# Attention: a tile's transposed probabilities gathered in SBUF, its products with V in one run beside the modulation's

## The chip, the cores and the metric

The kernel runs on one core of one Trainium2 chip. The metric is the device time of one execution in microseconds. The core has a matrix engine (TensorE, PE in the profile; PEld is its loading of the stationary operand), a vector engine (VectorE, DVE), a scalar engine (ScalarE, ACT), GpSimd (POOL) and SyncE (SP), which here issues DMAs. Matrix products land in PSUM, which has eight banks of 128 x 512 fp32; from there VectorE and ScalarE copy results to SBUF.

## The reference, cut to what matters

The program is one step of a diffusion transformer with two layers, on 128 context tokens and 1024 latent tokens. The part that the change touches is the attention of a layer and, beside it, the modulation, a product of the two conditioning vectors with a wide matrix.

```python
def block_attention(q, k, v):              # 8 heads, q and k 96 wide, v 64 wide
    def one_block(qi):                     # 128 queries at a time
        s = jnp.einsum('bqhd,bkhd->bhqk', qi, k).astype(F32) * scale
        p = jax.nn.softmax(s, axis=-1).astype(v.dtype)
        return jnp.einsum('bhqk,bkhd->bqhd', p, v)
...
def layer(x, cond, lp, rope=None, ctx=None):
    mod = (jax.nn.silu(cond) @ lp['w_ada'] + lp['b_ada'])[:, None, :]
    sh1, sc1, g1, sh2, sc2, g2 = jnp.split(mod, N_MOD, axis=-1)
    h = rmsnorm(x, lp['g_mix']) * (1 + sc1) + sh1
    comb = h @ lp['w_in']
    attn, ckv, kr = mla_mixer(comb[..., :MLA_IN], lp, rope, None if ctx is None else ctx[:2])
    ...
    mixed = jnp.concatenate([attn, ssm, conv], axis=-1)
    x = x + g1 * (mixed @ lp['w_out'])
```

Context queries see the 128 context keys alone; latent queries see 128 cached and 1024 latent keys. The scan (`ssm`) and a long convolution over 31 tokens (`conv`) are the other two mixers of the layer.

## The kernel before

The kernel holds the 1152 tokens in three chunks of 384, features on the partitions. A layer runs its input projections and the scan, then the attention, the output projection and the feed-forward part. Accurate products are made of three matmuls in a reduced fp32 format (`mm3`, lines 103 to 105: high by high, high by low, low by high); the products with V, the modulation's and the transposes are plain fp32.

The attention runs over four pairs of heads (`i`) and, in each, nine tiles of 128 queries (`t`). Tile 0 holds the context queries and has one block of 128 keys; the other eight, called full here, have three blocks of 384 keys (nine times 128). For each of the two heads of a pair (`j`), `scores` makes the blocks of scores in banks of the tag "A" (five), takes their maximum on VectorE (line 806), joins the maxima (808) and scales them (809), and writes the exponentials with their sums to `P` on ScalarE (811). `attend`, run for a tile while the next one's scores are made, takes the keys two times 128 at a time: it transposes the four blocks of P on TensorE (832) to a bank "T" (two), copies them to `pt` on ScalarE or VectorE (837 and 839), and multiplies them with V into the only bank "V" (843), both heads side by side on 64 columns each. At its end a product with ones (854) spreads the reciprocal sums, and VectorE scales the result into `mo` (857), which goes to DRAM.

Spread over the tiles of layer 0 are the steps of the modulation (`adas`, line 166): a load of 512 KB of w_ada on SP's queue into a ring `ws` of three buffers, two steps ahead of its use, and eight products of 32 columns (186), whose results are added up in `ms` on VectorE. They show in the trace as 16 passes, as each plain fp32 product takes two; a product with V does too. The taps of the long convolution (`conv_taps`) run on GpSimd through both attentions, and `conv_norm` (line 875; its first matmuls are on line 881) reads their result from tile 25 on. `prep_k`, `prep_v`, `prep_r` and `prep_q` make a pair's keys, values and queries from the latents.

The calls stand in the loops in one order, but the framework schedules: each engine's queue is filled from what is ready by the framework's own estimate of time, the work that is earlier in the text first. On the chip every queue then runs strictly in that order. So a step of the modulation, for example, is cut in two where an older product becomes ready.

Of the kernel before, what the change touches and what calls it, by code (L numbers as in the profile page):

```python
# [8 lines left out]
F32 = mybir.dt.float32  # L9
# [8 lines left out]
KD = 8  # L18
# [35 lines left out]
def build(tc, nc, ap, dbg=None):  # L54
# [109 lines left out]
    KO = (0, 4, 1, 5, 2, 6, 3, 7)  # L164

    def adas(rounds, stage=None, ahead=2):
        """128 columns of each of a round's four quarters at a time; loads run ahead of the products"""
        stage = stage or wp
        steps = [(l, r, q, k) for l, r in rounds for q in range(4) for k in range(0, KD, 2)]
        loads = []  # L170
        m = None
        for n in range(len(steps) + ahead):
            if n < len(steps):
                l, r, q, k = steps[n]
                loads.append(stage.tile([128, 1024], F32, tag="ws", name="ws", bufs=ahead + 1))
                Q.dma_start(loads[-1], ap["w_ada"][l, r, q, k // 2])
            if n >= ahead:
                l, r, q, k = steps[n - ahead]
                st = loads.pop(0)
                if k == 0:  # L180
                    m = sm.tile([128, 128], F32, tag="ms", name="ms", bufs=2)
                b = bank("A")
                for kk in range(2):
                    for j in range(4):
                        o = 512 * kk + 128 * j
                        PE.matmul(b[32 * j:32 * j + 32, :128], cond[:, k + kk, :], st[:, o:o + 128],
                                  start=kk == 0, stop=kk == 1)
                if k:
                    add_to(V, m, b[:, :128], m)
                else:  # L190
                    copy(m, b[:, :128])
                if k == KD - 2:
                    ada_end(l, r, q, m)
            yield
# [25 lines left out]
    def norm_r(x, p, sqs=None):  # L220
        """1 / rms of the chunk's tokens on every partition; sqs: room for all squares, summed on TensorE"""
# [72 lines left out]
    first = adas([(0, 0)], sp, 6)  # L294
# [15 lines left out]
    for l in range(L):  # L310
# [6 lines left out]
        def h_terms(c, w):  # L317
            """stationary weights [k, cols], moving h chunk"""
# [4 lines left out]
        # ================= in projection: x, B, C of the scan =================  # L323
# [17 lines left out]
        for c in range(NC3):  # L341
# [34 lines left out]
        # lowest: what the attention's first tiles can take over soonest  # L376
# [6 lines left out]
        # ================= state-space scan =================  # L383
        # dt = softplus(.), log1p(e) = 2 atanh(e / (2 + e))
# [89 lines left out]
        def ssd_out():  # L474
# [12 lines left out]
            for c in range(9):  # L487
                o = xcol(c)
                # dt of the pairs of tokens in each direction's range
# [13 lines left out]
                # a direction's exponents are 0 outside of its range  # L503
# [10 lines left out]
                if c == 8:  # L514
                    # the long convolution's products would hold up the scan on this engine
# [39 lines left out]
        # ================= in projection: conv module =================  # L555
# [28 lines left out]
        def latent(c):  # L584
            """chunk c's query latent (high and low part, halves), key latent (high and low part), rotary key"""
# [35 lines left out]
        def token_tail(c, tns, ss):  # L621
            # rotary key part
# [57 lines left out]
        def latents():  # L680
            # cached keys
# [27 lines left out]
        def prep_v(r, cs=range(NC3)):  # L709
# [3 lines left out]
            for c in cs:  # L713
                ck = lat[c][1]
                for t in range(KC[c][0] // 128, KC[c][1] // 128):
                    b0 = bank("A")
                    o = 128 * t - KC[c][0]
                    mm3(b0[:, :256], [(ck[:, 0, o:o + 128], ck[:, 1, o:o + 128],
                                       w[0][:, 512 + 256 * r:768 + 256 * r], w[1][:, 512 + 256 * r:768 + 256 * r])])
                    copy(vt[r][:, t], b0[:, :256])  # L720

        def prep_k(i, cs=range(NC3)):
            w = lat["w"][0]
            for c in cs:
                a, b = KC[c]
                b0 = bank("A")
# [15 lines left out]
        # ================= attention =================  # L742
        qr = {}

        def prep_r(r, cs=range(NC3)):
            if r not in qr:
                qr[r] = at.tile([128, T], F32, tag="qr", name="qr", bufs=1)
            for c in cs:
                tb = [at.tile([128, CH], F32, tag="tb", name="tb", bufs=4) for _ in range(2)]
                for n in range(2):  # L750
                    Q.dma_start(tb[n], ap["rf"][:, c, n])
                    b0 = bank("A")
                    o = 512 * n + 128 * r
                    mm3(b0[:, :CH], [(wr[0][:, o + 256 * k:o + 256 * k + 128], wr[1][:, o + 256 * k:o + 256 * k + 128],
                                      lat[c][0][:, 0, k], lat[c][0][:, 1, k]) for k in range(2)])
                    V.tensor_mul(tb[n], tb[n], b0[:, :CH])
                add_to(V, qr[r][:, CH * c:CH * c + CH], tb[0], tb[1])
# [4 lines left out]
        prep_r(0, (0, 1))  # L762
        prep_k(0, (2,))
        prep_v(0, (2,))
        prep_r(0, (2,))
# [19 lines left out]
        class Tile_:  # L785
            """one tile of queries of a pair of heads"""

            def __init__(self, i, t, q, mo):
                self.i, self.t, self.q, self.mo = i, t, q, mo
                self.sl = small(8, "sl", 3)  # L790
                self.prs = []

            def scores(self, j):
                """exp of a head's scores, less their maximum, and the sums"""
                t, q, sl = self.t, self.q[j], self.sl
                o = 128 * (t % 3)
                blocks = [(0, 128)] if t == 0 else [(128 + CH * b, CH) for b in range(3)]
                n = len(blocks)
# [3 lines left out]
                for b, (k0, w) in enumerate(blocks):  # L802
# [4 lines left out]
                if n > 1:  # L807
                    V.reduce_max(mx[:, 3:4], mx[:, 0:3], axis=AX.X)
                V.tensor_scalar_mul(mx[:, 3:4], mx[:, 3:4] if n > 1 else mx[:, 0:1], -SCALE)  # L809
                for b, (k0, w) in enumerate(blocks):  # L810
                    S.activation(pr[:, CH * b:CH * b + w], bs[b][:, :w], AF.Exp, bias=mx[:, 3:4], scale=SCALE,  # L811
# [369 lines left out]
```

## Time and profile before

| what | us |
|---|---|
| median of 3 runs | 3323.62 |
| lowest and highest of them | 3323.19, 3326.77 |
| span of the profiled execution | 3325.1 |
| of it: layer 0's attention, first score to the output projection (346.9 to 763) | 416.1 |
| of it: layer 1's attention (2005 to 2360) | 355.0 |

The span of the profiled execution, from its first to its last instruction, lies within the three runs and 1.5 us above their median. In the rows further down, a row of the timeline gives the start of an instruction, or of a merged run of equal ones (x8 is eight), and the modelled time up to the end of the last. Matmuls overlap in the array, so their durations exceed the distance between their starts; what one costs is the distance from its start to the start of the next.

### The profile page before, as it was taken

The numbers are of one execution on the slowest core, as the hardware profiler recorded it, in microseconds if no ns is written. First come the engines' busy times: TensorE is split into PE (matmuls) and PEld (weight loads), VectorE is DVE, ScalarE is ACT, GpSimd is POOL, SyncE is SP. The second block draws the span as 40 slices with busy tenths as digits, with TensorE's granted clock in tenths as the row PEclk, the third lists the DMA queues.
The fourth block names the chain that finished last, engine by engine and source line by source line (L and its number), as shares of the span: only waits on it lengthen the run. The fifth ranks groups of instructions, "written<-read, shape, count | busy, mean of one in ns | idle before, by whom it ended". The sixth has DMA issues, their size and how long they took to land. (4 is left out here: it accounts for less than half of the span.)

```text
span 3325.1 us, 50558 instructions
## 1 busy us (share of the span) xinstructions
PE 3123.8 (94%) x20610; PEld 2900.9 (87%) x20610; DVE 1856.9 (56%) x3811; ACT 1081.1 (33%) x2461; POOL 1183.7 (36%) x699
## 2 busy tenths in 40 slices
PE   6995799999999999999999957999999999999998
PEld 5974667779999999999999746777899999999997
DVE  6779876663733333333386798777463333333335
ACT  4433455563411111111143334667431111111113
POOL 2457994012412112111233579672232212112112
PEclk7997899999999999999999978999999999999998
DMA  6100333334111111111121010000311111111111
GB/s 233 54 24 31 115 113 122 125 132 146 29 48 45 45 39 45 45 39 39 51 100 54 24 49 18 11 17 30 137 39 39 45 45 45 45 39 45 45 32 58
DMA packets 67000, 202.36 MB, mean 61 GB/s; under 512 B 7888, under 2 KB 25424, under 8 KB 65232
## 3 DMA queue, kind: packets, MB, share of 16 engines
q1 hardware_dynamic: 63456, 194.02, 17.5%
q10 hardware_dynamic: 3312, 5.11, 0.4%
q8 instruction: 162, 2.65, 0.3%
q14 instruction: 70, 0.57, 0.1%
HBM read 177.44 MB, written 21.66 MB: 60 GB/s over the span
## 5 line engine op out<-in xcount | busy, mean ns | idle before, releaser
L81 POOL TENSOR_TENSOR wl<-ws,wh 128x1024 fp32r<-128x1024 f32 x164 | 399.1, 2440 | 1581.0 <-ACT wh L84 1508.5
L103 PE MATMUL psA<-hh,wh 128*128 128x384 f32 x2496 | 836.6, 337 | 4.4 <-ACT hh L270 2.7
L104 PE MATMUL psA<-hl,wh 128*128 128x384 f32 x2496 | 837.5, 336 | 0.4 <-DVE hl L271 0.4
L105 PE MATMUL psA<-hh,wl 128*128 128x384 f32 x2496 | 837.5, 336 | 0.0
L103 PEld LDWEIGHTS psA<-hh,wh 128*128 128x128 f32 x2496 | 471.4, 189 | 8.5 <-ACT hh L270 3.9
L104 PEld LDWEIGHTS psA<-hl,wh 128*128 128x128 f32 x2496 | 471.6, 189 | 2.2 <-DVE hl L271 1.1
L105 PEld LDWEIGHTS psA<-hh,wl 128*128 128x128 f32 x2496 | 471.3, 189 | 0.3
L998 DVE TENSOR_TENSOR fs<-fs,psA 128x384 f32<-128x384 f32 x132 | 72.9, 554 | 666.5 <-PE psA L105 657.6
L78 POOL TENSOR_TENSOR acc<-ct,acc 128x1167 f32<-128x1167 f32 x120 | 326.5, 2720 | 9.8
L84 ACT ACTIVATE wh<-ws 128x1024 fp32r<-128x1024 f32 (+1 forms) x178 | 184.5, 1049 | 414.7 <-PE psA L104 197.4
L997 ACT ACTIVATE fs<-psA 128x384 f32<-128x384 f32 x132 | 63.8, 485 | 655.6 <-PE psA L105 655.6
L1051 DVE SCALAR_TENSOR_TENSOR x<-psT,mod,x 128x384 f32<-128x384 f32 (+1 forms) x320 | 157.7, 513 | 198.6 <-PE psT L105 198.6
L811 ACT ACTIVATE P<-psA,mx 128x384 f32<-128x384 f32 (+1 forms) x400 | 224.1, 571 | 132.8 <-DVE mx L809 87.8
L806 DVE TENSOR_REDUCE mx<-psA 128x1 f32<-128x384 f32 (+1 forms) x400 | 209.0, 540 | 78.2 <-PE psA L105 75.7
L1051 DVE SCALAR_TENSOR_TENSOR x<-psA,mod,x 128x384 f32<-128x384 f32 (+2 forms) x384 | 186.8, 513 | 53.4 <-PE psA L105 46.9
L1001 DVE TENSOR_TENSOR fl<-fs,fh 128x384 fp32r<-128x384 f32 x132 | 167.5, 1270 | 65.7 <-ACT fh L84 65.7
L843 PE MATMUL psV<-pt,vv 128*64 128x128 f32 x2336 | 191.5, 285 | 5.4 <-DVE pt L837 2.8
L832 PE MATMUL psT<-cst,P 128*128 128x128 f32 x1168 | 193.9, 287 | 2.4 <-DVE mod L203 1.0
L104 PE MATMUL psA<-fl,wh 128*128 128x384 f32 x576 | 193.2, 335 | 0.0
L105 PE MATMUL psA<-fh,wl 128*128 128x384 f32 x576 | 193.0, 335 | 0.0
L103 PE MATMUL psA<-fh,wh 128*128 128x384 f32 x576 | 189.9, 337 | 2.7 <-DVE fs L998 2.7
L103 PE MATMUL psA<-K,q 128*128 128x384 f32 (+1 forms) x400 | 160.6, 402 | 28.2 <-ACT P L811 21.5
(267 smaller groups left out, 6020.1 us busy)
## 6 DMA issues: line engine op xcount, KB each, us to landing
ws<-w_ada SPq DMA_DIRECT2D x96, 512.0 KB, 3.4
ws<-w_gate SPq DMA_DIRECT2D x44, 512.0 KB, 3.6
ws<-w_up SPq DMA_DIRECT2D x44, 512.0 KB, 3.5
ws<-w_down SPq DMA_DIRECT2D x44, 512.0 KB, 3.5
x<-xT SPq DMA_DIRECT2D x6, 1536.0 KB, 7.8
ws<-w_fm SPq DMA_DIRECT2D x16, 512.0 KB, 3.4
ws<-w_out SPq DMA_DIRECT2D x16, 512.0 KB, 3.6
mf<-mixed SPq DMA_DIRECT2D x18, 384.0 KB, 5.7
```

The lines of the kernel that those rows point to most:

```text
L78: eng.tensor_tensor(out, a, b, ALU.add)
L81: eng.tensor_tensor(out, x, hi.bitcast(F32), ALU.subtract)
L84: S.activation(out, x, AF.Copy)
L103: PE.matmul(out, sh, mh, start=i == 0, stop=False)
L104: PE.matmul(out, sh, ml, start=False, stop=False)
L105: PE.matmul(out, sl, mh, start=False, stop=i == n - 1)
L806: V.reduce_max(mx[:, b:b + 1], b0[:, :w], axis=AX.X)
L811: S.activation(pr[:, CH * b:CH * b + w], bs[b][:, :w], AF.Exp, bias=mx[:, 3:4], scale=SCALE, accum_out=sl[:, 3 * j + b:3 * j + b + 1])
L832: PE.transpose(tb[:, 256 * u + 128 * j:256 * u + 128 * j + 128], prs[j][:, 128 * (a + u):128 * (a + u) + 128], ident)
L843: PE.matmul(ob[64 * j:64 * j + 64, :128], vv[:, kt, 64 * h:64 * h + 64], pt[:, 256 * u + 128 * j:256 * u + 128 * j + 128], start=kt == kts ...
L1001: V.tensor_sub(fl[:, sl], sg, fh[:, sl].bitcast(F32))
L1051: V.scalar_tensor_tensor(X[c][:, m, a:b], b0[:, a:b], modT[l][:, 40 + m, s:s + 1], X[c][:, m, a:b], ALU.mult, ALU.add)
```

## The change

`attend` is parted. `turn` makes the 18 transposes of a full tile in five groups and keeps them all in one buffer `pt` (128 x 2 x 1152); its groups are placed behind the second and third score block of each head of the next tile, and what is left of it behind that tile's scores. Then `attend` makes the tile's 36 passes with V and the sums' product, which now writes columns 256 to 383 of the same bank "V". `P` has three buffers for four, `pt` one for three smaller ones.

`adas` takes two loads and 16 products a step in the attention (40 steps for 80), issues the next loads behind the products, and is called behind `attend`: twice at every third tile, once at the others. `prep_q` for a pair's first chunk comes at the last tile of the pair before, `prep_r(1)` in three parts in pair 1, `prep_v` copies two tiles from one bank. Comments are dropped. Cut to its core:

```diff
-    def adas(rounds, stage=None, ahead=2):
+    def adas(rounds, stage=None, ahead=1, per=2):
+        steps = [(l, r, q, k) for l, r in rounds for q in range(4) for k in range(0, KD, 2 * per)]
...
+        def load(l, r, q, k):
+            bufs = 3 if stage is None else ahead + 1
+            sts = [(stage or wp).tile([128, 1024], F32, tag="ws", name="ws", bufs=bufs) for _ in range(per)]
+            for i, st in enumerate(sts):
+                Q.dma_start(st, ap["w_ada"][l, r, q, k // 2 + i])
+            loads.append(sts)
...
+            for kk in range(2 * per):
+                for j in range(4):
+                    o = 512 * (kk % 2) + 128 * j
+                    PE.matmul(b[32 * j:32 * j + 32, :128], cond[:, k + kk, :], sts[kk // 2][:, o:o + 128],
+                              start=kk == 0, stop=kk == 2 * per - 1)
...
+            if stage is None and n + ahead < len(steps):
+                load(*steps[n + ahead])
...
-    first = adas([(0, 0)], sp, 6)
+    first = adas([(0, 0)], sp, 6, 1)
...
-                pr = at.tile([128, T], F32, tag="P", name="P", bufs=4)
+                pr = at.tile([128, T], F32, tag="P", name="P", bufs=3)
...
+            def turn(self):
+                self.pt = at.tile([128, 2, T], F32, tag="pt", name="pt", bufs=1)
+                todo = [(j, u) for u in range(len(self.kts)) for j in range(2)]
+                pt = self.pt.rearrange("p j (u q) -> p u j q", q=128)
+                for a in range(0, len(todo), 4):
+                    part = todo[a:a + 4]
+                    tb = bank("T")
+                    for n, (j, u) in enumerate(part):
+                        PE.transpose(tb[:, 128 * n:128 * n + 128], self.pr[j][:, 128 * u:128 * u + 128], ident)
...
+                    if a % 8:
+                        V.tensor_copy(o, src)
+                    else:
+                        copy(o, src)
+                    yield
             def attend(self):
...
+                for u, kt in enumerate(self.kts):
+                    for j in range(2):
+                        h = 2 * (i % 2) + j
+                        PE.matmul(ob[64 * j:64 * j + 64, :128], vv[:, kt, 64 * h:64 * h + 64],
+                                  self.pt[:, j, 128 * u:128 * u + 128], start=u == 0, stop=u == n - 1)
...
                 for j in range(2):
-                    PE.matmul(rb[64 * j:64 * j + 64, :128], ones[:, 0:64], dl[:, j], start=True, stop=True)
+                    PE.matmul(ob[64 * j:64 * j + 64, 256:384], ones[:, 0:64], self.dl[:, j], start=True, stop=True)
...
                     cur = Tile_(i, t, qs[i, c], mo)
-                    cur.scores(0)
...
-                    next(ag, None)
-                    next(prev, None)
-                    cur.scores(1)
-                    next(ag, None)
-                    drain(prev)
-                    prev = cur.attend()
+                    for j in range(2):
+                        for b, _ in enumerate(cur.scores(j)):
+                            if b:
+                                next(turn, None)
+                    drain(turn)
+                    if prev:
+                        prev.attend()
+                    for _ in range(2 if t % 3 == 0 else 1):
+                        next(ag, None)
+                    prev, turn = cur, cur.turn()
                     if t == 3 * c and c + 1 < NC3:
                         qs[i, c + 1] = prep_q(i, c + 1)
-                    if t % 2:
-                        next(ag, None)
+                    if i == 1 and t >= 5 and t < 8:
+                        prep_r(1, t - 5)
+                    if t == 8 and i + 1 < NPAIR:
+                        qs[i + 1, 0] = prep_q(i + 1, 0)
```

## Rows read from the trace of the kernel before

**Rows 1.** The page's part 1: busy time, share of the span and instructions.

```profile
PE 3123.8 (94%) x20610; PEld 2900.9 (87%) x20610; DVE 1856.9 (56%) x3811; ACT 1081.1 (33%) x2461; POOL 1183.7 (36%) x699
```

**Rows 2.** Busy time by stretch: stretch, length, engines' busy us, granted clock, DMA.

```profile
346.90:763.00 416.10, 391.75 (x3995) 299.68 (x3995) 296.33 (x763) 228.55 (x652) 195.17 (x97) 0.98 0.37 127
...
2005.00:2360.00 355.00, 325.95 (x2695) 265.65 (x2695) 269.90 (x671) 224.81 (x632) 199.65 (x98) 0.98 0.08 28
```

**Rows 3.** TensorE's timeline, layer 1: start us, modelled us, instruction, count.

```profile
2253.64 1.09 PE L843 MATMUL psV<-pt,vv 128*64 128x128 f32 x16
2254.67 0.66 PE L832 MATMUL psT<-cst,P 128*128 128x128 f32 x4
2255.26 0.66 PE L843 MATMUL psV<-pt,vv 128*64 128x128 f32 x8
2255.84 0.44 PE L832 MATMUL psT<-cst,P 128*128 128x128 f32 x2
...
2256.30 0.33 PE L104 MATMUL psA<-K,q 128*128 128x384 f32 x1
2256.47 0.33 PE L105 MATMUL psA<-K,q 128*128 128x384 f32 x1
...
2257.51 0.34 PE L105 MATMUL psA<-K,q 128*128 128x384 f32 x1
2257.77 0.66 PE L843 MATMUL psV<-pt,vv 128*64 128x128 f32 x8
2258.26 0.39 PE L854 MATMUL psT<-dl,ones 128*64 128x128 f32 x4
...
2258.80 1.09 PE L832 MATMUL psT<-cst,P 128*128 128x128 f32 x8
2259.65 0.42 PE L103 MATMUL psA<-K,q 128*128 128x384 f32 x1
...
2260.62 0.34 PE L105 MATMUL psA<-K,q 128*128 128x384 f32 x1
2260.80 0.60 PE L832 MATMUL psT<-cst,P 128*128 128x128 f32 x4
2261.15 0.48 PE L103 MATMUL psA<-lat,wh 128*128 128x512 f32 x1
```

**Rows 4.** The same view, layer 0, where modulation stands beside V.

```profile
678.60 0.66 PE L843 MATMUL psV<-pt,vv 128*64 128x128 f32 x8
679.19 0.64 PE L186 MATMUL psA<-ws,cond 128*32 128x128 f32 x16
679.76 0.66 PE L832 MATMUL psT<-cst,P 128*128 128x128 f32 x4
```

**Rows 5.** By line: count, least/median/most ns, first and last start; layers 0 and 1.

```profile
L186 PE MATMUL psA<-ws,cond x1280: 272/273/423, 359.3 to 722.8; 128*32 128x128 f32 x183
...
L843 PE MATMUL psV<-pt,vv x1168: 272/273/324, 2017.0 to 2358.5; 128*64 128x128 f32 x195
```

**Rows 6.** Waits of TensorE in layer 1's stretch: us in total, times, longest.

```profile
PEld psA L103 <- ACT P L811: 19.8, 16, 3.3
```

**Rows 7.** Timeline: GpSimd's last tap in layer 1, and its reader.

```profile
2254.24 2.68 POOL L78 TENSOR_TENSOR acc<-ct,acc 128x1167 f32<-128x1167 f32 x1
...
2267.98 1.25 PE L881 MATMUL psA<-acc,ones 128*128 128x128 f32 x6
```

**Rows 8.** DMA issues of 500 to 700 us: count, KB each, median us to landing.

```profile
ws<-w_ada SPq DMA_DIRECT2D x44, 512.0 KB, 3.3
```

**Rows 9.** Groups of 500 to 700 us: count, busy us, mean ns, idle time before.

```profile
L811 ACT ACTIVATE P<-psA,mx 128x384 f32<-128x384 f32 x97 | 55.3, 580 | 42.3 <-PE psT L832 26.5 <-DVE mx L809 15.6
L806 DVE TENSOR_REDUCE mx<-psA 128x1 f32<-128x384 f32 x96 | 51.5, 552 | 22.3 <-PE psA L105 21.6
...
L811 ACT ACTIVATION_READ_ACCUMULATOR P<-psA,mx 128x1 f32 x100 | 20.4, 204 | 0.0
...
L809 DVE TENSOR_SCALAR mx<-mx 128x1 f32<-128x1 f32 x36 | 5.4, 150 | 0.7
```

More of the change, by code (lines that the diff above doesn't have):

```diff
@@ L164, in build @@
     KO = (0, 4, 1, 5, 2, 6, 3, 7)
-    def adas(rounds, stage=None, ahead=2):
-        stage = stage or wp
-        steps = [(l, r, q, k) for l, r in rounds for q in range(4) for k in range(0, KD, 2)]
+    def adas(rounds, stage=None, ahead=1, per=2):
+        steps = [(l, r, q, k) for l, r in rounds for q in range(4) for k in range(0, KD, 2 * per)]
         loads = []
         m = None
[L172 to L193, printed above, removed]
@@ new lines, in load @@
+        def load(l, r, q, k):
[4 more added lines that the diff above has]
+            loads.append(sts)
+        for s in steps[:ahead]:
+            load(*s)
+            if stage is not None:
+                yield
+        for n, (l, r, q, k) in enumerate(steps):
+            if stage is not None and n + ahead < len(steps):
+                load(*steps[n + ahead])
+            sts = loads.pop(0)
+            if k == 0:
+                m = sm.tile([128, 128], F32, tag="ms", name="ms", bufs=2)
+            b = bank("A")
+            for kk in range(2 * per):
[3 more added lines that the diff above has]
+                              start=kk == 0, stop=kk == 2 * per - 1)
+            if k:
+                add_to(V, m, b[:, :128], m)
+            else:
+                copy(m, b[:, :128])
+            if stage is None and n + ahead < len(steps):
+                load(*steps[n + ahead])
+            if k == KD - 2 * per:
+                ada_end(l, r, q, m)
@@ L743, in build, with prep_r @@
         qr = {}
-        def prep_r(r, cs=range(NC3)):
+        def prep_r(r, c):
             if r not in qr:
                 qr[r] = at.tile([128, T], F32, tag="qr", name="qr", bufs=1)
[L748 to L757, printed above, removed]
+            tb = [at.tile([128, CH], F32, tag="tb", name="tb", bufs=4) for _ in range(2)]
+            for n, b0 in enumerate([bank("A") for _ in range(2)]):
+                Q.dma_start(tb[n], ap["rf"][:, c, n])
+                o = 512 * n + 128 * r
+                mm3(b0[:, :CH], [(wr[0][:, o + 256 * k:o + 256 * k + 128], wr[1][:, o + 256 * k:o + 256 * k + 128],
+                                  lat[c][0][:, 0, k], lat[c][0][:, 1, k]) for k in range(2)])
+                V.tensor_mul(tb[n], tb[n], b0[:, :CH])
+            add_to(V, qr[r][:, CH * c:CH * c + CH], tb[0], tb[1])
         drain(so)
@@ L789, in __init__ @@
                 self.i, self.t, self.q, self.mo = i, t, q, mo
+                self.blocks = [(0, 128)] if t == 0 else [(128 + CH * b, CH) for b in range(3)]
+                self.kts = [0] if t == 0 else list(range(1, 10))
                 self.sl = small(8, "sl", 3)
-                self.prs = []
+                self.pr = []
             def scores(self, j):
@@ L796, in scores @@
                 o = 128 * (t % 3)
-                blocks = [(0, 128)] if t == 0 else [(128 + CH * b, CH) for b in range(3)]
-                n = len(blocks)
-                pr = at.tile([128, T], F32, tag="P", name="P", bufs=4)
+                n = len(self.blocks)
+                pr = at.tile([128, T], F32, tag="P", name="P", bufs=3)
+                self.pr.append(pr)
                 mx = small(4, "mx", 3)
                 bs = []
-                for b, (k0, w) in enumerate(blocks):
+                for b, (k0, w) in enumerate(self.blocks):
                     b0 = bank("A")
```

95 lines of the change are left out of this document (43 added, 52 removed).

## Prediction, made before the result was known

> **What bounds the kernel now.** I read the page first, then the windows of the two attention stretches, then TensorE's timeline inside them. TensorE is busy for 94% of the span [rows 1]. The change lies in the two attention stretches, 416.1 us in layer 0 and 355.0 us in layer 1 [rows 2], so the question is what these are made of. In both, TensorE counts as busy for over nine tenths, VectorE for 71 and 76%, ScalarE for 55 and 63%. A busy share is no rate, because the matmuls are pipelined, so I went to the start times in the timeline.
>
> There the steps are almost constant [rows 3]. A score matmul of 384 columns starts 0.17 us after the one before (2256.30 to 2256.47). Eight transposes up to the next score block take 0.85 us (2258.80 to 2259.65), 0.106 each. Sixteen passes of the product with V take 1.03 us (2253.64 to 2254.67) and eight take 0.58 (2255.26 to 2255.84): eight more cost 0.45, or 0.056 a pass, and each run carries 0.13 us beyond its passes. Four transposes ahead of V take 0.59 (2254.67 to 2255.26), four ahead of a projection of K 0.35 (2260.80 to 2261.15): 0.24 us more for the way into V. A score matmul ahead of V takes 0.26 (2257.51 to 2257.77) where 0.17 is usual, and a score matmul ahead of a transpose 0.18 (2260.62 to 2260.80). Where V is followed by the matmul of the sums, which also writes 64 columns of the array, eight passes take only 0.49 (2257.77 to 2258.26).
>
> So transposes among score blocks cost next to nothing, and each change between work on 128 columns (scores, transposes, projections) and work on 64 (V, sums) or 32 (modulation) costs 0.1 to 0.2 us. V to modulation is such a change too: its eight passes take 0.59 (678.60 to 679.19), not 0.49, and the modulation's 16 passes ahead of a transpose 0.57 [rows 4].
>
> Counted along the same timeline, from the first to the last row that [rows 5] names, layer 1 has 125 unbroken runs of 64-column work and 249 changes of width; layer 0 has 142 such runs, 80 of the modulation and 422 changes. At the rates above the work alone would fill 308 us of layer 0's stretch and 273 us of layer 1's. Starts more than 0.45 us apart (waits) account for 27 and 32 us. What is left, 80 and 50 us, is 0.19 and 0.20 us a change; in 500 to 700 us, where there is hardly a wait, it is 0.17. I take **0.17 us for a change**.
>
> **The change part by part.**
>
> *Products with V in one go.* A full tile has 18 transposes and 36 passes with V before and after; none is removed. Before, transposes and products alternate in groups, about 3.5 runs of V and sums a tile in layer 1. Now the transposes stand between score blocks, where they cost nothing, and V's 36 passes and the 4 of the sums follow in one piece. The order on the engine is the scheduler's, which places whatever is ready: in the trace a modulation step of 16 passes is often cut by V's. I therefore don't count one run a tile but 1.5. Layer 1: 36 tiles give 54 runs and 108 changes, 141 fewer than 249, at 0.17 us **24 us**.
>
> *Modulation in 40 steps of 32 passes for 80 of 16, behind V.* The passes stay. I count 54 runs of V and 40 of the modulation, half of which touch a run of V and so share a change: 2 x 94 - 20 = 168 changes for 422, 254 fewer, **43 us**. VectorE's additions into ms fall from 60 to 20, off the path, and so count for nothing. A rule speaks against the last words of the change: the Trainium skill, TensorEngine Tiling (Array Packing), Key Properties, says that a change of tiling mode, not only of tile, drains the engine. By it, modulation beside V still pays; the trace agrees, 0.59 against 0.49. Had standing side by side been free, as by the number format alone it might, 20 more changes would go, 3.4 us; I count them as paid.
>
> *The queues the modulation is moved past.* Each step now takes two loads of 512 KB from a ring of three buffers, issued on SP behind the step before. The first finds a free buffer; the second waits until the preceding step has read its first half. A load lands 3.3 us after its issue [rows 8]. With one step a tile that is hidden under a tile (11.6 us in layer 0). At every third tile two steps follow at once, about ten times: there the second half of the second step is 3.3 us late, minus what runs meanwhile. Between nothing (the scheduler puts score blocks there) and 33 us; I take nothing, since those blocks are ready. Behind the waiting load on SP stand only the stores of mo and loads of rf, for which nothing is late.
>
> *Smaller buffers.* P has 3 buffers for 4, pt one for three. The second head's exponentials must now wait for the last transposes of the tile before, and they are queued ahead of copies on ScalarE. In the trace the wait of score blocks for banks that exponentials hold is 19.8 us in layer 1 [rows 6]; of P's own ring no row shows a wait. From no cost to that of the rival below; I take half of 19.8, **10 us lost**, for both layers, as denser TensorE work also leaves VectorE and ScalarE less slack.
>
> *Preparation.* The rotary queries of pair 2 and each pair's first queries are made a tile or more earlier, and V's preparation copies two tiles at once. The passes are the same; the cover they need (transposes and products of the last tile) is at hand. Zero, from -5 to +5 us: what stalls of this sort there are now is a few us.
>
> *A bound in layer 1.* The convolution on GpSimd runs without a break and ends at 2256.9 (2254.24 + 2.68); the matmul that needs its second half starts at 2267.98 [rows 7]. It is 11 us late today. If TensorE's order stays, only 11 us can be gained before that row; 96 of the 141 changes, 16 us, lie ahead of it. So layer 1 gives 11 + 8 = **19 us**. In layer 0 the convolution ends far ahead of its reader.
>
> **Sum:** 43 + 19 - 10 = 52 us. The profiled span is 3325.1 us, 1.5 above the median of the runs, so 3273 for a span and **3272 us** for the median.
>
> **Rivals.** *The clean order*: one run a tile, all of the 40 steps next to V. Then layer 0 has 2 x (36 + 40) - 36 = 116 changes and layer 1 has 72: 306 + 177 fewer, 82 us, and if score blocks wait less for banks because transposes now stand between them, up to 10 more: 3325 - 92 = 3233. For it: V's inputs are ready together. Against it: the scheduler cuts, and GpSimd's bound.
>
> *The gain is taken back by VectorE and ScalarE*, or the order stays cut (2.5 runs a tile, 60 modulation runs: 191 changes fewer, 32 us) with 20 us of new waits: about 3312. For it: VectorE is busy 270 of 355 us in layer 1 and TensorE's work alone is 273.
>
> *Slower: the ring of P.* One mechanism: the second head's exponentials wait for the last transposes, these for a bank copied on ScalarE behind the first head's exponentials. Until they run, three of the five score banks are held, and the next tile's third block has none. From the third block's maximum to the first free bank it takes 0.55 (maximum) + 0.15 + 0.15 (two short steps on mx; one row stands for both) + 0.58 (exponential) + 0.20 (the read of its sum), about 1.7 us with the handoffs [rows 9]. The cover is V's run of 40 passes, 2.2 us; where the scheduler has put V earlier, nothing is left to cover it. There are 64 full tiles; the gain of 62 us is 0.97 a tile, so it decides from the point at which more than 57% of them pay the 1.7. If all pay and hand on another 0.3 us, 128 - 62 = 66 us slower: near 3390; at three in four, 3345. Against it: ScalarE is idle for over a third of both stretches.
>
> That the runs don't merge at all is the far end of the second rival: 3320 to 3325.
>
> **How the numbers follow.** Forecast (3245 to 3300) 0.60; clean order 0.13; taken back 0.15, half of it under 3315; slower 0.12. The range that leaves 2 in 10 out runs from 3236, most of the clean order, to 3318, all but the end of the second rival. A measurement of this kernel can tell about 0.2%, 6.6 us, from no change. Faster: 0.60 + 0.13 + 0.06 = 0.79; within 0.2%: 0.08; slower: 0.13.
>
> **What would show it.** Right: in TensorE's timeline runs of V of 20 passes and more, 64-column runs down from 125 and 142 towards 54 each, modulation runs from 80 to about 40; layer 0's stretch near 375 us and layer 1's near 335. The transposes stand between score blocks at 0.11 us each. If the 11 us bound holds, TensorE waits for GpSimd once in layer 1. Wrong: score blocks that wait for exponentials far above 19.8 us, or TensorE waiting for the load of w_ada; or changes that cost the same time when they are fewer, so that 0.17 was not their price.

## The result, and the profile after

The changed kernel takes 3368.3 us (median of 4 runs, 3362.37 to 3368.75). Against runs of the kernel before on the same chip that is a ratio of 1.0132, with an interval of 1.0117 to 1.0147: it is **slower by 1.3%**, where 52 us less had been forecast. The profiled execution has a span of 3366.7 us, 41.6 longer than before.

The engines' busy time answers [rows 1]: 3 us more on TensorE, 40 instructions fewer on VectorE (the additions), and otherwise nearly the same work.

```profile
PE 3127.0 (93%) x20610; PEld 2907.9 (86%) x20610; DVE 1862.8 (55%) x3771; ACT 1081.8 (32%) x2443; POOL 1184.4 (35%) x699
```

The windows of the two attention stretches answer [rows 2]; the columns are the same. Layer 0 went from 416.1 to 430.0 us and layer 1 from 355.0 to 379.1, together 38 of the 41.6 us.

```profile
349.70:779.70 430.00, 387.77 (x3996) 307.28 (x3996) 291.71 (x724) 230.12 (x648) 191.98 (x95) 0.96 0.36 123
...
2022.10:2401.20 379.10, 334.13 (x2696) 266.19 (x2696) 275.32 (x672) 225.25 (x627) 199.21 (x98) 0.98 0.08 27
```

TensorE's timeline in layer 1 answers [rows 3]: start, modelled duration, instruction, count, and in brackets a wait and what ended it.

```profile
2200.08 0.60 PE L851 MATMUL psT<-cst,P 128*128 128x128 f32 x4
2200.61 0.66 PE L868 MATMUL psV<-pt,vv 128*64 128x128 f32 x8
2201.72 0.66 PE L851 MATMUL psT<-cst,P 128*128 128x128 f32 x4 [0.46 <-DVE pt L855]
2202.31 0.66 PE L868 MATMUL psV<-pt,vv 128*64 128x128 f32 x8
2202.90 0.44 PE L851 MATMUL psT<-cst,P 128*128 128x128 f32 x2
2203.26 0.66 PE L868 MATMUL psV<-pt,vv 128*64 128x128 f32 x8
2203.85 0.45 PE L103 MATMUL psA<-K,q 128*128 128x384 f32 x1
```

This is not one go. Each eight passes of V start when the copy of their four blocks has landed, with transposes between them, as in the kernel before. In layer 1, 105 of the 142 unbroken runs of 64-column work have eight passes; in the kernel before it was 55 of 125.

The waits of TensorE's weight queue (in whole, times, longest) answer [rows 6] for layer 1. The first two rows are of the kernel before, the next four of the changed one:

```profile
PEld psT L832 <- ACT P L811: 0.8, 1, 0.8
...
PEld psT L832 <- DVE pt L837: 0.2, 1, 0.2
```

```profile
PEld psA L103 <- ACT P L828: 13.0, 15, 2.1
PEld psT L851 <- ACT P L828: 12.4, 15, 1.8
...
PEld psT L851 <- DVE pt L855: 8.8, 12, 1.6
...
PEld psT L851 <- ACT pt L84: 3.5, 7, 0.7
```

In layer 1, score blocks wait less for exponentials than before (13.0 for 19.8 us). It is the transposes that now wait, 24.7 us for 1.0: for exponentials, and for the copies to `pt` that set the banks "T" free. In layer 0 two other waits stand beside these: the transposes of the modulation's sums `ms` wait for VectorE's additions, and V waits for the scaling into `mo`. The kernel before has 4.4 us of waits of a score block for `ms` there and none of V for `mo`. The last row answers the question of w_ada's late load [rows 8].

```profile
PEld psT L208 <- DVE ms L78: 7.4, 10, 2.8
PEld psV L868 <- DVE mo L875: 6.4, 2, 3.6
...
PEld psA L193 <- DMA ws<-w_ada: 0.4, 1, 0.4
```

In the experiments below (e1 to e16) I split the two stretches as the prediction did: the work alone (312.0 us in layer 0 and 274.8 in layer 1, by the start distances, the same in each kernel with this work; the prediction had 308 and 273), the waits (start distances above 0.45 us, less 0.2) and the rest, which is the changes of width and whatever the clock takes. "At 1.2 GHz" is the time in both stretches in which the granted clock was at the lower of its two levels, summed over rows of windows. From the stretches on, a row comes from one profiled execution. The ratio is taken against runs of the kernel before on the same chip, a chip for each set (the changed kernel; e1 to e4; e5 to e8; e9 to e12; e13 to e16). The medians of these runs lie between 3316.9 and 3323.4 us, so between sets the ratios say more than differences of medians do.

| kernel | median us | ratio, 95% | layer 0, layer 1 us | changes | waits us | rest us | at 1.2 GHz us |
|---|---|---|---|---|---|---|---|
| before | 3323.4 | | 416.4, 355.0 | 422, 249 | 28.9, 33.1 | 75.4, 47.1 | 37.5 |
| after | 3368.3 | 1.0132 [1.0117, 1.0147] | 430.0, 379.0 | 339, 283 | 47.3, 49.3 | 70.7, 54.9 | 44.3 |
| e1 | 3349.9 | 1.0085 [1.0065, 1.0104] | 426.4, 371.9 | 185, 79 | 64.5, 65.1 | 50.0, 32.0 | 61.7 |
| e2 | 3368.1 | 1.0141 [1.0125, 1.0156] | 426.2, 387.1 | 349, 283 | 42.7, 53.3 | 71.5, 59.0 | 61.5 |
| e3 | 3351.2 | 1.0088 [1.0072, 1.0103] | 423.7, 366.5 | 178, 79 | 61.6, 57.9 | 50.1, 33.8 | 58.3 |
| e4 | 3363.8 | 1.0135 [1.0116, 1.0154] | 423.1, 382.8 | 349, 283 | 42.9, 52.1 | 68.2, 55.9 | 40.9 |
| e7 | 3329.7 | 1.0031 [1.0019, 1.0043] | 402.5, 363.3 | 214, 79 | 41.3, 58.0 | 49.2, 30.6 | 41.2 |
| e8 | 3332.5 | 1.0044 [1.0027, 1.0062] | 403.8, 364.5 | 332, 183 | 28.9, 49.3 | 62.9, 40.4 | 44.3 |
| e9 | 3337.9 | 1.0054 [1.0037, 1.0071] | 425.6, 357.1 | 402, 249 | 35.4, 36.2 | 78.2, 46.1 | 54.8 |
| e12 | 3315.6 | 0.9986 [0.9975, 0.9997] | 405.3, 351.6 | 332, 249 | 30.5, 31.2 | 62.8, 45.6 | 34.3 |
| e15 | 3312.5 | 0.9985 [0.9974, 0.9996] | 407.7, 348.6 | 448, 315 | 22.4, 22.0 | 73.2, 51.8 | 13.6 |
| e16 | 3301.7 | 0.9951 [0.9932, 0.9969] | 395.3, 348.0 | 225, 71 | 36.0, 45.5 | 47.3, 27.7 | 34.3 |

So the change, as made, saved 83 changes of width in layer 0, added 34 in layer 1, and brought 18 and 16 us of new waits.

### The profile page after: what moved, and what is told of

Same layout as the page of the kernel before. It is cut to its first block, busy times and chain, and to the rows that moved or that the text cites. A ratio compares the mean times of both kernels' runs of the same rounds, so it can differ in the third digit from the quotient of the medians.

```text
span 3366.7 us, 50305 instructions
## 1 busy us (share of the span) xinstructions
PE 3127.0 (93%) x20610; PEld 2907.9 (86%) x20610; DVE 1862.8 (55%) x3771; ACT 1081.8 (32%) x2443; POOL 1184.4 (35%) x699
## 4 chain that ended last, share of the span: by engine, by line
PE 75%; DVE 17%; ACT 3%; issue 3%; DMA 2%; POOL 0%; SPq 0%; ACTq 0%; DVEq 0%; POOLq 0%
PE psA L103 20%; PE psA L104 19%; PE psA L105 19%; PE psV L868 4%; PE psT L851 3%; PE psT L103 2%; PE psT L104 2%; PE psT L105 2%; DVE mx L822 2%; DVE dl L839 1%; DVE q L795 1%; ACT P L828 1%; PE psA L193 1%; DVE rt L150 1%; DVE nu L279 1%
## 5 line engine op out<-in xcount | busy, mean ns | idle before, releaser
L851 PE MATMUL psT<-cst,P 128*128 128x128 f32 x1168 | 202.2, 285 | 30.6 <-DVE pt L855 12.1
L851 PEld LDWEIGHTS psT<-cst,P 128*128 128x128 f32 x1168 | 136.6, 142 | 74.7 <-issue 22.1
```

The lines of the kernel that those rows point to most:

```text
L851: PE.transpose(tb[:, 128 * n:128 * n + 128], self.pr[j][:, 128 * u:128 * u + 128], ident)
```

## The experiments

My theory after these views was that the scheduler cuts V, so that the change pays for the waits of transposes queued ahead of V and gets little of its saving. The rivals: the smaller ring of P or the one large `pt` makes the waits; the modulation or the preparation does; or V in one piece is itself the slower order.

### V forced into one run (e1), and the ring of P (e2, e3)

Nothing in the kernel keeps V's products together: each is ready when its own block has been copied. In e1 they begin with the block pair that is copied last, so that none can start early.

```diff
-                for u, kt in enumerate(self.kts):
+                us = [n - 1] + list(range(n - 1))
+                for u in us:
+                    kt = self.kts[u]
...
-                                  self.pt[:, j, 128 * u:128 * u + 128], start=u == 0, stop=u == n - 1)
+                                  self.pt[:, j, 128 * u:128 * u + 128], start=u == us[0], stop=u == us[-1])
```

> The changed kernel, except that a full tile's products with V begin with the pair of blocks that is copied to SBUF last (u = 8), so that the scheduler cannot start the run before all copies are there. Theory A (the runs stayed cut, 129 and 142 runs of 64-column work and 340 and 284 changes of width; that is why the gain did not come): 64-column runs fall to about 60 and 45, changes to about 200 and 100, some 320 fewer, at 0.17 us 55 us: 3313 us. Theory B (the smaller rings of P and pt make the engines wait, whatever the order): the runs merge, but the waits of TensorE stay or grow by 10 to 30 us, since V's products can no longer fill them: 3340 to 3370 us.

e2 gives `P` its fourth buffer back and takes one of `rs` (`bufs=3` to 4, 2 to 1); e3 is both edits.

> The changed kernel with four buffers of P for three, as before the change (rs has one buffer for two to make room). Theory B: the second head's exponentials no longer wait for the last transposes of the tile before; waits of score blocks and transposes for exponentials (25 us in layer 1) fall to less than half, and of the 38 us that waits over 0.45 us grew, 20 to 30 go: 3340 us. Theory A: the runs stay cut, 3360 to 3370 us.

> Both edits: V begins with the last pair of blocks, and P has four buffers (rs one). Theory A: 3313 us or a little less, as without the fourth buffer. Theory B: 3330 to 3340 us, as with the fourth buffer alone. If both causes hold, their sum: about 3290 us.

e1 did what the change says: 32 and 29 runs of 40 passes, and 358 changes fewer than in the changed kernel. The rest fell by 43.6 us, 0.12 a change. But the waits rose by 33 us, and the median fell only 18, to 3349.9, still slower than before: the range of theory B, though not by its rings, as e2 and e3 show below. TensorE's timeline of e1, layer 1, and ScalarE's of the same stretch show how (in this tile V's run is cut after 28 passes):

```profile
2138.48 1.04 PE L851 MATMUL psT<-cst,P 128*128 128x128 f32 x8
2139.76 0.44 PE L851 MATMUL psT<-cst,P 128*128 128x128 f32 x2 [0.25 <-ACT pt L84]
2140.68 1.75 PE L870 MATMUL psV<-pt,vv 128*64 128x128 f32 x28 [0.47 <-ACT pt L84]
2142.35 0.45 PE L103 MATMUL psA<-K,q 128*128 128x384 f32 x1
```

```profile
2139.11 0.60 ACT L84 ACTIVATE pt<-psT 128x512 f32<-128x512 f32 x1 [0.71 <-PE psT L851]
2140.24 0.38 ACT L84 ACTIVATE pt<-psT 128x256 f32<-128x256 f32 x1 [0.53 <-PE psT L851]
2140.65 0.58 ACT L828 ACTIVATE P<-psA,mx 128x384 f32<-128x384 f32 x1
```

Where transposes and V alternate, V's eight passes run while the next copy is made. In one run there is no such cover: the two banks "T" are full, the transposes wait for a copy, and V for the last one. The waits of e1's layer 1 (rows as above) have all three kinds:

```profile
PEld psA L103 <- ACT P L828: 21.8, 29, 3.8
PEld psT L851 <- ACT pt L84: 12.0, 20, 1.7
PEld psT L851 <- ACT P L828: 11.2, 10, 1.9
PEld psT L851 <- DVE pt L855: 11.1, 8, 2.2
```

The ring of P is not it: e2 takes what the changed kernel takes (3368.1), e3 what e1 takes (3351.2).

### Smaller copies in a ring (e4)

e4 gives the changed kernel six buffers `pt` of 128 x 512, one for each group, so that a group's copy need not wait for the tile before.

> The changed kernel, with pt in six buffers of 128 x 512, one for each group of transposes, in place of one buffer for the whole tile; P keeps three. Theory C (the single pt holds the next tile's first copies until the last product with V of the tile before): waits of transposes for copies of pt (7.5 and 8.8 us) go, and with them the transposes that stand behind: 10 to 20 us, 3350 us. Theories A and B: no difference beyond 7 us.

3363.8 us, 1.0135 [1.0116, 1.0154]: the one large `pt` costs nothing that shows. The waits of transposes for copies in layer 1, which theory C had going, stay (13.3 us for 12.3).

### Both kernels in the order of their text (e5, e6)

The order on the engines is the framework's, by its estimate of time. e5 is the kernel before and e6 the changed one, both without that estimate, so that work is taken in the framework's plain order.

```diff
-TileContext(nc, schedule_with_timeline_sim=True)
+TileContext(nc, schedule_with_timeline_sim=False)
```

> The kernel before the change, each engine's queue filled by the framework's plain order, without its estimate of time. Theory D (the scheduler's estimate of time, in which changes of width cost nothing, and not the text, decides how the work stands on TensorE): the order becomes that of the text, four transposes and eight products with V in turn, and TensorE waits for each copy: 3450 us or more. Theory E (the order follows the text anyway): within 20 us of the kernel before, 3322.

> The changed kernel, likewise without the estimate of time. Theory D: V stands in one run of 40 passes a tile, 64-column runs near 40 to 50 a layer; what the change gains over the kernel before shows only here, at least 60 us less than the kernel before in the same plain order. Theory E: 3360 us, as the changed kernel with the estimate.

e5 takes 3480.35 us (ratio 1.0487 [1.0468, 1.0507]) and e6 3459.9 (1.043 [1.0402, 1.0459]). Both lose far more outside the attention than the change is about, but beside each other they show that in the same plain order **the change gains 20 us**: layer 0 from 421.6 to 405.5 us, layer 1 from 384.7 to 370.1 (the rest of the kernel gives 13 us of that back). The changes fell from 446 and 283 to 272 and 205, and the waits of both layers together from 79.1 to 74.6 us. The loss of the real pair therefore hangs on the order in which the work is queued. It is a third of the 60 us expected, and V did not stand in one piece here either: 106 and 103 runs of 64-column work, where 40 to 50 a layer were expected.

### The transposes' places (e7, e13, e14)

e7 is e3 with the first two groups of a tile's transposes one score block later; e13 is the changed kernel with that edit alone. The condition below skips the second block of the first head and adds the first block of the second, so the third and fourth groups stay where they were, although the expectations say "each group".

```diff
-                            if b:
+                            if b + 3 * j > 1:
```

e14 is e1 with the groups at the places of the kernel before (three behind the first head's scores, the others behind the second's).

```diff
-                        for b, _ in enumerate(cur.scores(j)):
-                            if b:
-                                next(turn, None)
+                        drain(cur.scores(j))
+                        for _ in range(3 - 3 * j):
+                            next(turn, None)
```

> The changed kernel with V begun by the last pair of blocks and P in four buffers (as e3), and each group of transposes one score block later: behind the third block of the first head and each block of the second. Theory F (the first group of transposes stands too close behind the exponentials of the tile before: 1.0 us of score blocks after V's run where 1.6 us and more stood before): waits of transposes for P and for copies, 40 to 45 us in e1, fall by half: 3325 to 3335 us. If the waits come from something else (ScalarE's copies behind the next exponentials, say), 3345 to 3355 us.

> The changed kernel with each group of transposes one score block later and nothing else (V's runs stay cut, P keeps three buffers). If the places alone make the waits: layer 1 falls from 379 by 15 us or more, all in all 3340 to 3350 us. If it took V's one run as well: 3360 to 3370 us.

> The changed kernel with V begun by the last pair of blocks (as e1) and the transposes where they stood before the change: three groups behind the first head's three blocks, two behind the second's, then V. If the places make the waits: waits over 0.45 us fall from e1's 130 us to 80 or less, 3300 to 3315 us. If they come with V's one run, whatever the places: 3340 to 3350 us, as e1.

e7 takes 3329.7 us, 21 less than e3 by the medians and 19 by the ratios, whose intervals lie apart. In its profile (of the lowest of its ten runs, 3319.9 us) the gain is in layer 0, with 20 us less of waits (those of transposes for VectorE's copies fell from 15.9 to 5.5 us). In layer 1, with the same 79 changes, the waits stay at 58 us: those of transposes for exponentials fell from 7.7 to 1.5 us, those of V for ScalarE's copies rose from 5.8 to 12.1. e14 takes 3337.1 (1.0056 [1.0039, 1.0073]), 13 less than e1 by the medians and 10 by the ratios, with intervals that overlap; its waits are 110 us for 130. e13 takes 3354.3 (1.0113 [1.0095, 1.013]), 14 less than the changed kernel by the medians but 6 by the ratios, again with overlap, and its profile shows none of it in the attention: layer 0 fell from 430.0 to 425.4 us, layer 1 rose from 379.0 to 383.8, where a fall of 15 was expected. So with V in one run the place of the first groups is worth some 20 us, in layer 0; with V cut it is not shown to be worth anything. A group that has to wait holds up all that is queued on TensorE behind it. No place tried brought the merged order below the kernel before.

### Two runs instead of one (e8, e12)

The kernel before with the products of the first three groups of a tile together (24 passes) and the last two together (12), each half beginning with the group copied last; its ring of three `pt` is enough for that. e12 does it in layer 0 alone.

```diff
-                for a in range(0, len(kts), 2):
+                for half in ((0, 2, 4), (6, 8)):
+                    pts = {}
+                    for a in half:
...
+                        pts[a] = pt
+                    order = sorted(pts)[-1:] + sorted(pts)[:-1]
+                    for a in order:
...
```

> The kernel before, except that a tile's products with V stand in two runs for five: three groups of transposes, then their 24 passes beginning with the group copied last, then two groups and their 12 passes. P, pt, the modulation and the sums as before. If the price of a change of width (0.12 us by e1, 0.17 by my prediction) is real and only the new places of the transposes make the waits: 64-column runs fall from 125 and 142 to about 75 and 90, some 200 changes fewer, 25 to 35 us: 3290 to 3300 us. If merging V itself brings the waits: 3320 to 3340 us.

> The kernel before with two runs of V a tile in layer 0 alone (there e8 fell from 416 to 404 us, while layer 1 rose from 355 to 365); layer 1 as before. If the layers' results add: 404 + 355 us, 12 us less than the kernel before, 3305 us. If a layer's stretch varies by 10 us with any new order that the scheduler makes, nothing of it needs to return: 3305 to 3325 us.

e8 lost 0.44% in all, but its layers went apart: layer 0 fell from 416.4 to 403.8 us with unchanged waits (28.9), layer 1 rose from 355.0 to 364.5 with 16 us more of them. My reading, which no run isolates, is that in layer 0 the modulation's passes cover the copies, while layer 1 has none. Hence e12, which keeps the old order in layer 1: 3315.6 us over 10 runs, 0.9986 [0.9975, 0.9997]. It beats both kernels, the one before by 0.14% only, 5 us where 12 were expected if the layers' results add.

### The modulation and the preparation (e9, e10, e11)

e9 is the kernel before with the modulation alone changed (40 steps, behind the products with V). e10 and e11 are the changed kernel with the old modulation (80 steps, still called behind the products with V), and with the old preparation of keys, values and queries.

```diff
                     drain(prev)
+                    for _ in range(2 if t % 3 == 0 else 1):
+                        next(ag, None)
```

> The kernel before with the modulation's part of the change alone: 40 steps of two loads and 32 passes, called behind a tile's products, twice at every third tile. If the modulation's part is sound: changes of width in layer 0 fall from 422 to about 340 and layer 0's stretch from 416 by 10 us; 3305 to 3310 us. If the late second load and a bank held longer cost it: layer 0 416 to 425 us, TensorE waits for w_ada several us; 3320 to 3325 us. Layer 1 has no modulation and stays at 355 us.

> The changed kernel with the modulation in 80 steps as before, called two or three times behind a tile's products. If the modulation's part of the change is sound, this is slower than the changed kernel: layer 0 430 to 440 us; 3370 to 3380 us. If it carries the loss in layer 0: layer 0 near 416 us, 3352 us. Layer 1 as in the changed kernel, 379 us, within the scatter of a schedule.

> The changed kernel with the preparation of keys, values and queries as before the change. If the loss comes from the places of the transposes, as e7 suggests: layer 1 within 6 us of 379, 3360 to 3370 us. If the earlier preparation crowds VectorE and ScalarE: layer 1 near 365 us, 3345 to 3355 us.

e9 takes 3337.9 us (1.0054 [1.0037, 1.0071]), e10 and e11 no less than the changed kernel by the ratios (3363.0, 1.0139 [1.0124, 1.0154], and 3368.2, 1.0158 [1.0143, 1.0173]). So e9 is above both of its expected ranges, while e10 shows no cost of the 40 steps in the changed kernel: what they cost hangs on what stands around them. The modulation alone saved 20 changes, since its steps are cut (69 runs for 80), cost 6.5 us of waits in layer 0, and no wait on w_ada to speak of. It also has 17 us more at 1.2 GHz. The windows of e9, layer 0, show such a stretch: TensorE was busy for 4.6 of 8 us, the granted clock fell to 1.2 GHz within it (0.66 of full in the mean), and it came back only in the next.

```profile
393.00:403.00 10.00, 9.81 (x111) 8.12 (x110) 7.82 (x15) 5.40 (x17) 9.55 (x6) 1.00 0.43 141
403.00:411.00 8.00, 4.59 (x44) 3.46 (x43) 5.77 (x12) 3.95 (x12) 7.64 (x5) 0.66 0.01 3
411.00:421.00 10.00, 10.00 (x111) 7.95 (x111) 5.61 (x17) 4.62 (x15) 9.64 (x5) 0.93 0.34 105
```

### A shorter chain from scores to transposes (e15, e16)

Most of the waits that grew in layer 1 lie on one chain: scores, maximum, exponential, transposes, copy. To shorten it, e15 (the kernel before) and e16 (e1) take the maximum of the first block only. A softmax comes out the same whatever is subtracted, as long as no exponential overflows. The edit of e16:

```diff
-                    V.reduce_max(mx[:, b:b + 1], b0[:, :w], axis=AX.X)
+                    if b == 0:
+                        V.reduce_max(mx[:, 0:1], b0[:, :w], axis=AX.X)
...
-                        if n > 1:
-                            V.reduce_max(mx[:, 3:4], mx[:, 0:3], axis=AX.X)
-                        V.tensor_scalar_mul(mx[:, 3:4], mx[:, 3:4] if n > 1 else mx[:, 0:1], -SCALE)
+                        V.tensor_scalar_mul(mx[:, 3:4], mx[:, 0:1], -SCALE)
```

> The kernel before with the maximum of a head's first block of scores alone in place of that of all three: two of three maxima and their joining are left out, 1.2 us of VectorE a head, and the exponentials can start two blocks earlier. If the chain from scores to transposes is what TensorE waits for: waits fall from 62 us to below 35 and the time by 20 to 40 us, to 3280 to 3300 us. If TensorE's own work and its changes set the pace: 3305 to 3315 us.

> The changed kernel with V begun by the last pair of blocks (e1), and one maximum a head, as e15. If the chain ate up what the 358 changes fewer than in the changed kernel gave: it falls by 60 us or more against e1's 3350 and below e15, to 3250 to 3285 us. If waits come with the merged order for another reason (ScalarE's copies behind exponentials): about 3320 to 3335 us, above e15.

e15 takes 3312.5 us, 8 less than the kernel before beside it by the medians and 5 by the ratio: the range expected if TensorE's own work sets the pace, not the chain. Its waits fell from 62 to 44 us, with 92 changes more. e16 takes 3301.7, **48 less than e1** by the medians and 44 by the ratios. With the shorter chain, the merged order is the faster by 11 us, where with the full chain it was 0.85% the slower (e1). The edit also takes 22 to 24% of VectorE's busy time in the stretches away, and the two runs don't part the shorter chain from the emptier engine. The expectation for e16 was lower still; 81 us of waits are left, and in layer 1 they are mostly those of the transposes:

```profile
PEld psT L850 <- ACT pt L84: 13.6, 23, 1.0
PEld psT L850 <- DVE pt L854: 12.9, 18, 2.5
PEld psT L850 <- ACT P L827: 10.1, 14, 2.2
PEld psA L103 <- ACT P L827: 7.7, 9, 1.8
```

The wait of score blocks for exponentials is down from e1's 21.8 to 7.7 us; that of transposes for copies is not (26.5 for 23.1). Whether more banks "T" or copies ahead of the exponentials on ScalarE would take it was not tried.

## Why the prediction was wrong

**V in 1.5 runs a tile: the step that failed first.** The prediction knew that the order is the scheduler's and that it places what is ready, and still counted on 1.5 runs; what it had for merging is said under the clean order, that V's inputs are "ready together". They are ready one group at a time, behind a copy of 0.60 us on ScalarE or 0.69 on VectorE each, and in 105 of 142 runs a group's eight passes went in by themselves. Instead of 254 and 141 changes fewer there were 83 fewer and 34 more. At 0.13 to 0.17 us each that is a gain of 11 to 14 us in layer 0 and a loss of 4 to 6 in layer 1, where 43 and 24 were forecast; the measured rest, in which the clock has its share, moved by 4.7 down and 7.8 up. The modulation's "40 runs" failed in the same way: 63.

**"10 us lost" to waits: the step that failed as well, and with V in one run would have sunk the forecast alone.** The sum took the waits for a constant to which half of one row is added. That row fell (19.8 to 13.0 us in layer 1), and the waits came up elsewhere, before the transposes above all. In all they rose by 35 us in the changed kernel, with V cut, and by 68 in e1, with V in one run; 68 is more than the 62 us that the sum had as gain. The e1 row is the test of the idea itself: 407 changes fewer than before, for 395 in the forecast and 483 in "the clean order", and the kernel was still slower. A group of V between two groups of transposes does not only cost two changes; as the rows of e1 and of the changed kernel show, it also hides the copy that the second group's bank waits for. e8 shows the exchange in one kernel: in layer 0 merging by halves leaves the waits as they are and gains 12.6 us, in layer 1 it adds 16 us of them and loses 9.5.

**"Transposes among score blocks cost next to nothing."** True of the array, where a transpose takes 0.11 us and its neighbour no longer than usual [rows 3]. False of the queue: e7 moves two groups of the same transposes by one block and wins 19 to 21 us.

**0.17 us for a change** was about right, somewhat high. From after to e1, 358 changes fewer took 43.6 us off the rest, while the time at 1.2 GHz rose by 17.4 us, which costs up to half of that. So a change is worth 0.12 to 0.15 us. The Trainium skill, TensorEngine Tiling (Array Packing), Key Properties, says that a change of tiling mode drains the engine; the runs agree that a change costs, and e1's figure is their price for it.

**The rivals.** The slower one named the right side and a wrong mechanism: the ring of P is without effect (e2). Its place was near, as the waits do run through exponentials and copies on ScalarE, but the point is the banks "T" and the order, and a row pointed at it beforehand: in [rows 3] two of the four groups of transposes stand right behind eight or sixteen passes of V, and none shows a wait. "Taken back" had 20 us of new waits at 191 changes fewer; there were 35 at 49 fewer. Its far end, that the runs don't merge at all, is what came about, and the prediction priced it at 3320 to 3325 us, the kernel before without a new wait. Of the signs of being wrong that it named, neither wait came: score blocks wait less for exponentials than before, and TensorE hardly for w_ada.

**What held.** The second load of w_ada costs nothing in the changed kernel (0.4 us of waiting), the preparation nothing (e11, with the old one, is not faster). The bound by GpSimd never came to bear: the last tap ends at 2275.3 (2272.60 + 2.69), and its reader starts at 2288.86, 13.6 us behind it for the 11.1 of [rows 7], because TensorE became later, not earlier.

**What stays open.** How the 35 us of waits split between the banks "T", the places of the transposes and the modulation: e4, e10 and e13 each move parts of them by no more than the profiles of one order differ. Layer 1 with TensorE's same order took 379.0 (after), 382.8 (e4), 387.1 (e10) and 387.1 us (e2) in one execution each, so the verdicts above rest on the runs' times and ratios, not on one profile.

## What to carry to other kernels

Saving changes of an engine's mode pays only as far as the work between them was not the cover for something else: before merging runs, list for each instruction in the merged run which copy or bank it waits for, and what will stand in front of it. Where a framework orders the queues, "in one go" has to be enforced by a dependence (here: begin with what is ready last), and merging by halves, where there is cover, can win what merging in whole loses. The test of a merge is the sum of changes and waits, not the count of either.

## What the runs showed of the hardware

**The clock behind a wait.** In e1, layer 1, TensorE waits 2.10 us for a part of K (its timeline). The window that holds this wait has it busy for 5.9 of 8 us; in the 8 us behind it, where it was busy for 5.1 and waited 2.33 us once more (2123.05), the granted clock is at 1.2 GHz, and it comes back in the third:

```profile
2117.99 0.41 PE L104 MATMUL psA<-K,q 128*128 128x128 f32 x1 [2.10 <-DVE K L748]
```

```profile
2110.00:2118.00 8.00, 5.90 (x59) 4.88 (x58) 5.87 (x7) 5.15 (x14) 7.72 (x4) 0.92 0.01 2
2118.00:2126.00 8.00, 5.12 (x18) 4.28 (x19) 7.72 (x12) 3.29 (x7) 7.64 (x5) 0.51 0.00 1
2126.00:2134.00 8.00, 8.00 (x70) 7.55 (x70) 6.04 (x16) 4.21 (x15) 7.64 (x5) 0.85 0.00 0
```

Not every such stretch is followed by a fall. In e14, layer 1, TensorE was busy for 1.86 of the 4 us from 2238.20 on, and the granted clock is 1.00 there and in every 4 us row up to 2270.20. That the wait brings the fall is therefore not shown.

Four profiles with TensorE's same order in layer 1 (after, e4, e10, e2) show what it goes with: 13.7, 20.4, 27.3 and 30.9 us at 1.2 GHz stand beside 379.0, 382.8, 387.1 and 387.1 us, about half a microsecond for each, with the waits (49.3 to 53.3 us) differing too. By that, an estimate: of e9's loss of 15.4 us of span, up to 8.7 is of this kind (17.3 us more at the lower level), and of e15's gain perhaps most of it, as 23.9 us fewer there would give up to 12 of 15.7.

**VectorE beside GpSimd.** While GpSimd runs its taps, some operations of VectorE take twice their time; in the kernel before, layer 1, during the taps and after their end (groups by line: count, busy us, mean ns):

```profile
L837 DVE COPY pt<-psT 128x512 f32<-128x512 f32 x44 | 30.2, 687 | 22.6 <-PE psT L832 20.3 <-ACT P L811 1.8
L781 DVE SCALAR_TENSOR_TENSOR q<-qr,cst,q 64x384 fp32r<-64x384 f32 x20 | 27.8, 1391 | 0.5
L850 DVE TENSOR_TENSOR dl<-cst,sl 128x256 f32<-128x256 f32 x25 | 25.4, 1018 | 0.6
```

```profile
L837 DVE COPY pt<-psT 128x512 f32<-128x512 f32 x20 | 13.8, 688 | 8.2 <-PE psT L832 8.1
...
L850 DVE TENSOR_TENSOR dl<-cst,sl 128x256 f32<-128x256 f32 x10 | 4.2, 420 | 0.1
...
L781 DVE SCALAR_TENSOR_TENSOR q<-qr,cst,q 64x384 fp32r<-64x384 f32 x4 | 2.8, 690 | 0.1
```

Operations that read two tiles from SBUF go from 0.42 to 1.02 and from 0.69 to 1.39 us; the copy from a bank keeps its 0.69. The two slower ones stand in VectorE's queue among the maxima and the copies, so what is behind them there comes later, in both kernels alike; how much of the waits that makes, no run shows.
